# Second block, from mixing to feed-forward: work ordered by token tile

## The chip, the cores and the metric

The kernel runs on one core of one Trainium2 chip. The metric is the device time of one execution in microseconds, the median of several runs. TensorE (PE in the profile, PEld for its weight loads), VectorE (DVE), ScalarE (ACT) and GpSimd (POOL) compute; SyncE (SP) issues the transfers from the main memory.

## The reference

The program is two networks in a row on 256 tokens of width 1024. The first block (two layers with attention and a mixture of 32 experts) isn't touched. The second block ends like this, and only this part is touched:

```
merged = jnp.sum(gates * proj, axis=2)                 # (256, 1024)
x = x + rmsnorm(merged @ w_mix_out[l], post_mix_g[l])  # w_mix_out 1024 x 1024

h = rmsnorm(x, pre_ffn_g[l])
gt = causal_dwconv(h @ w_ff_gate[l], ff_conv_w[l]) + ff_conv_b[l]      # 1024 x 2816
y = (jax.nn.gelu(gt, approximate=True) * (h @ w_ff_up[l])) @ w_ff_down[l]
x = x + rmsnorm(y, post_ffn_g[l])
```

`rmsnorm(x, g)` is `x * rsqrt(mean(x * x) + 1e-6) * g`, over the 1024 features of each token. All of it is float32. The tokens are two tiles of 128, t = 0 and 1.

## The kernel before

**Split products.** A float32 matrix is split into a high part, rounded to the type float32r, and a low part, the rest (`split_into`, L266 for the cast on ACT and L269 for the subtraction on DVE or POOL). `mm` (L259 to L261) multiplies with three matmuls: high by high, high by low, low by high. Weights come as tiles of 1 MB (`W`, L302), which rotate through a ring of four. `W.tiles` splits such a tile into pieces of 128 x 1024, each into a pair of buffers of the pool `sp`; with six buffers three pairs rotate, and a pair is free again when its last matmul is through.

**Mixing.** `w_mix_out` is worked off in two halves of 512 columns. The merged activations `mT`, features on partitions, are the stationary operand and the weights move, 512 columns at a time: for each half 8 blocks k of 128 features, 2 token tiles, 3 matmuls, 96 in all, into four banks `pj`. In the second half `tail` asks for the blocks from the third on tile by tile: all of tile 0, then all of tile 1.

**The norms.** `post` takes the mean square of the four banks with Square on ACT (L1953), in the order half 0 tile 0, half 0 tile 1, half 1 tile 0, half 1 tile 1, then a root (L1955) and reciprocal (L1956) for each tile. For each tile DVE scales each half by that and by the gain row (L1963), and DVE or POOL adds it to X (L1964). Then each tile's X is squared (L1993); one root and one reciprocal serve both tiles (L1599, L1600). DVE writes X times that into `xn`, with the features re-ordered (L2000). `scaled_T` transposes it block by block on TensorE (L445), and ACT and DVE make from each transposed block, times the gain `g2`, the high and low part of `hT` (L1594, L1595).

**Feed-forward.** Six pieces of up to 512 columns of the gate and up weights in turn. In `fproj_g` the weights are the stationary operand, 128 columns at a time, and `hT` moves with all 256 tokens: 8 blocks k, 4 column groups, 3 matmuls, 96 a piece. Convolution and GELU follow on ACT and DVE, then the down projection, and `post` again, at the end of the program, with the output's transfers behind it.

**What sets the order.** The program is written as a plain sequence. A planner with its own model of the engines' times puts each engine's instructions into a queue: among the instructions that are ready in its reckoning it takes the one written first. TensorE, DVE and POOL follow the planner's queues; on ACT the instructions marked `pin` keep the written order among themselves. A tile of a pool that has the tag of another waits until that one's users are through.

Of the kernel before, what the change touches and what calls it, by code (L numbers as in the profile page):

```python
# [11 lines left out]
F32 = mybir.dt.float32  # L12
F32R = mybir.dt.float32r
# [5 lines left out]
D = 1024  # L19
# [144 lines left out]
def build(tc, A, out, stages=("A0", "M0", "A1", "M1", "F", "B"), dbg=None, inject=None):  # L164
# [22 lines left out]
    with es:  # L187
# [14 lines left out]
        def PS(tag="ps"):  # L202
            p, bufs = banks[-1]
            tag = one_bank[-1] if one_bank else tag
            tag = tag if tag in bufs else "ps"
            return p.tile([128, 512], F32, name=tag, tag=tag, bufs=bufs[tag])
# [5 lines left out]
        def pin(i, on=True):  # L212
            return tc.keep_in_program_order(i) if on and i is not None else i
# [235 lines left out]
        def t2(pool, dt=F32):  # L449
            return pool.tile([128, 512], dt, name="t2", tag="t2", bufs=t2n.get(id(pool), 6))  # L450
# [1094 lines left out]
        def block2():  # L1545
            with tc.tile_pool(name="blk", bufs=1, reuse_waits="tile") as B_, tc.tile_pool(name="splb", bufs=1, reuse_waits="tile") as sp:
                t2n[id(B_)] = 6
                esp = ExitStack()
                W.pools = [ringA] * 2 + [ringB] * (RN - 2)
                esp.enter_context(psum("ps_b1", ps=4, pj=4))  # L1550
# [393 lines left out]
                            if g == 2:  # L1944
                                split_into(mT[:, m:m + 2].rearrange("p a t -> p (a t)"), dst, pool_every=0)

                def post(row, pss, after, mid=lambda: None):
                    warm(AF.Sqrt)
                    ms = B_.tile([128, 2, 4], F32, name="pms", tag="pms", bufs=2)
                    for n in range(2):  # L1950
                        for t in range(2):
                            q0, q1, rs = (ms[:, t, i:i + 1] for i in range(3))
                            pin(S.activation(t2(B_), pss[t][n], AF.Square, accum_out=q1 if n else q0))  # L1953
                            if n:
                                pin(S.activation(rs, q1, AF.Sqrt, bias=q0, scale=1.0 / D))  # L1955
                                V.reciprocal(rs, rs)  # L1956
                            else:
                                V.tensor_scalar(q0, q0, 1.0 / D, 1e-6, op0=OP.mult, op1=OP.add)
                    for t in range(2):
                        for n in range(2):  # L1960
                            tmp = t2(B_)
                            cs = slice(512 * n, 512 * n + 512)
                            V.scalar_tensor_tensor(tmp, pss[t][n], ms[:, t, 2:3], row[:, cs], op0=OP.mult, op1=OP.mult)  # L1963
                            (V if n else G).tensor_add(X[:, t, cs], X[:, t, cs], tmp)  # L1964
                    mid()
                    for t in range(2):
                        after(t)

                def tail(lhs, parts, kn, last):
                    parts = list(parts)  # L1970
                    for late in range(2):
                        for t in range(2) if late else (None,):
                            for k, wk, cols in parts:
                                if (k >= kn - last) == late:
                                    for u in range(2) if t is None else (t,):
                                        for ps, cs in cols:
                                            mm(ps[u], lhs[:, k, 128 * u:128 * u + 128], wk[:, cs], k == 0, k == kn - 1)

                wm = A["w_mix_out_2"][0].rearrange("(k p) n -> p k n", p=128)
                row = L_.tile([128, D], F32, name="prow")  # L1980
                Q.dma_start(row, A["post_mix_g_2"].to_broadcast([128, D]))
                pss = []
                for n in range(2):
                    pss.append([PS("pj"), PS("pj")])
                    tail(mT, [(k, wk, [(pss[n], slice(0, 512))]) for k, wk in W(wm[:, :, 512 * n:512 * n + 512], 4).splits(sp)], 8, 6 * n)
                wfg = A["w_ff_gate_2"][0].rearrange("(p k) n -> p k n", k=8)
                wfu = A["w_ff_up_2"][0].rearrange("(p k) n -> p k n", k=8)
                xn = X[:, 2:4].rearrange("p t (k a) -> p t k a", k=8)
                ms = B_.tile([128, 2, 2], F32, name="nms")
                gate0 = W(wfg[:, :, 0:512], 4)  # L1990

                def after(t):
                    pin(S.activation(xn[:, t].rearrange("p a b -> p (a b)"), X[:, t], AF.Square, accum_out=ms[:, 0, t:t + 1]))  # L1993

                gate0.start(sp, 1)
                post(row, [[pss[n][t] for n in range(2)] for t in range(2)], after)
                inv_rms(ms[:, 1], ms[:, 0], 1.0 / D)
                gate0.more(1)
                for t in range(2):
                    V.tensor_scalar(xn[:, t], X[:, t].rearrange("q (p k) -> q k p", k=8), ms[:, 1, t:t + 1], None, op0=OP.mult)  # L2000
                debug("xmix", X)
                es2.close()
                L_ = es2.enter_context(tc.tile_pool(name="ffn", bufs=1, reuse_waits="tile"))
                hT = scaled_T(1, xn)
                yF = s2tile(L_, [128, 22, 256], "yF")
                for c in range(6):
                    n = min(512, 2816 - 512 * c)
                    pgs = fproj(W(wfg[:, :, 512 * c:512 * c + n], 4) if c else gate0, n)
                    pus = fproj(W(wfu[:, :, 512 * c:512 * c + n], 4), n)
                    for b in range(n // 256):  # L2010
                        pg, pu = pgs[b], pus[b]
                        y = t2(B_)
                        for a in range(2):
                            f = 4 * c + 2 * b + a
                            ya, ga = y[:, 256 * a:256 * a + 256], pg[:, 256 * a:256 * a + 256]
                            S.activation(ya, ga, AF.Identity, bias=vcol(66 + f), scale=vcol(44 + f))
                            V.scalar_tensor_tensor(ya[:, 1:], ga[:, :255], vcol(22 + f), ya[:, 1:], op0=OP.mult, op1=OP.add)
                            V.scalar_tensor_tensor(ya[:, 2:], ga[:, :254], vcol(f), ya[:, 2:], op0=OP.mult, op1=OP.add)
                        S.activation(y, y, AF.Gelu_apprx_tanh)
                        f = 4 * c + 2 * b  # L2020
                        V.tensor_mul(y, y, pu)
                        split_into(yF[:, f:f + 2].rearrange("p a t -> p (a t)"), y, pool_every=1)
                wd = A["w_ff_down_2"][0].rearrange("(k p) n -> p k n", p=128)
                row = L_.tile([128, D], F32, name="prow")
                Q.dma_start(row, A["post_ffn_g_2"].to_broadcast([128, D]))
                pss = [[PS("pj"), PS("pj")] for _ in range(2)]
                cols = [(pss[n], slice(512 * n, 512 * n + 512)) for n in range(2)]
# [106 lines left out]
```

## Time and profile before

| | |
|---|---|
| median of 3 runs | 2079.9 us (2075.26 to 2083.57) |
| profiled execution, own time | 2082.3 us |
| its span | 2080.6 us |
| mean granted TensorE clock | 0.975 |
| PE busy in the span | 1944.3 us (93%) |
| DVE / ACT / POOL busy | 1076.9 / 658.5 / 475.8 us |
| the second block, about | 1512 to the end |
| mixing matmuls end / first gate matmul | 1870.0 / 1883.5 us |

Times in the views are microseconds from the start of the span. A row of a timeline gives start, duration, engine, line, operation, what it writes and reads, shape, count, and in brackets how long the engine was idle before it and what ended that. The end of a matmul is modelled, and neighbouring matmuls overlap; their rate is read from start to start. Some matmul records are missing, so counts can be a little low.

### The profile page before, as it was taken

Reading aid. Unit: us, or ns where it says so; the run is one execution under the profiler, and the core shown is the slowest. Engines: PE = TensorE matmul, PEld = TensorE weight load, DVE = VectorE, ACT = ScalarE, POOL = GpSimd, SP = SyncE. Lnnn points to the kernel's source line nnn. Section 1 sums busy time; section 2 is a strip of 40 time slices with the busy share of each in tenths; the row PEclk is TensorE's granted clock in tenths of the full one; section 3 lists DMA queues with packets and bytes.
Section 4 is the critical chain, followed back from the end, with each engine's and each line's share of the span. In section 5 each row is a group of like instructions: output and inputs, shape, how many; then the busy total and the mean of one; then the engine's idle time right before and its main releaser. Section 6 shows DMA issues by size and latency. Waiting matters only on the chain. (4 is left out here: it accounts for less than half of the span.)

```text
span 2080.6 us, 29614 instructions
## 1 busy us (share of the span) xinstructions
PE 1944.3 (93%) x11353; PEld 1229.8 (59%) x11353; DVE 1076.9 (52%) x1919; ACT 658.5 (32%) x1188; POOL 475.8 (23%) x365
## 2 busy tenths in 40 slices
PE   6999999999899998999899997999989999998997
PEld 3755574444344444677743332333379998988996
DVE  3476674454426566746643231233366775446553
ACT  3355531101001114446511010111164444455553
POOL 1234321121213123210111010011131440332331
PEclk7999999999999999999899999999999999999999
DMA  8573338999999996642389999999864453554552
GB/s 316 209 258 128 102 134 339 398 427 426 427 426 425 427 423 251 246 142 102 132 364 427 426 427 427 426 426 427 370 223 135 146 182 129 183 192 142 183 189 95
DMA packets 137794, 585.44 MB, mean 281 GB/s; under 512 B 17257, under 2 KB 21863, under 8 KB 88367
## 3 DMA queue, kind: packets, MB, share of 16 engines
q1 hardware_dynamic: 136798, 583.47, 71.8%
q8 instruction: 92, 1.51, 0.3%
q14 instruction: 56, 0.45, 0.1%
q10 hardware_dynamic: 848, 0.01, 0.0%
HBM read 582.33 MB, written 1.11 MB: 280 GB/s over the span
## 5 line engine op out<-in xcount | busy, mean ns | idle before, releaser
L1216 PE MATMUL ps<-w,xt 128*64 128x512 f32 (+1 forms) x2232 | 430.1, 612 | 23.7 <-DMA w<-expert_w 23.4
L269 DVE TENSOR_TENSOR spl<-w,sph 128x1024 fp32r<-128x1024 f32 (+1 forms) x153 | 203.8, 1335 | 193.8 <-ACT sph L266 192.7
L266 ACT CAST sph<-w 128x1024 fp32r<-128x1024 f32 (+1 forms) x204 | 213.0, 1045 | 282.0 <-PE pj L260 258.2
L1216 PEld LDWEIGHTS ps<-w,xt 128*64 128x64 f32 (+1 forms) x2232 | 125.6, 127 | 276.0 <-issue 225.1
L1271 DVE SCALAR_TENSOR_TENSOR t<-ps,gt,t 128x512 fp32r<-128x512 f32 x52 | 39.1, 751 | 474.7 <-ACT t L1270 473.0
L1255 PE MATMUL ps<-w,t 128*64 128x512 f32 (+1 forms) x1128 | 257.1, 604 | 16.3 <-DMA w<-expert_w 13.5
L1287 POOL TENSOR_TENSOR X<-X,tm 128x512 f32<-128x512 f32 x78 | 106.1, 1360 | 687.8 <-DVE tm L1286 686.5
L259 PE MATMUL pj<-hT2h,sph 128*128 128x256 f32 x864 | 241.0, 283 | 0.0
L260 PE MATMUL pj<-hT2l,sph 128*128 128x256 f32 x864 | 240.4, 280 | 0.0
L261 PE MATMUL pj<-hT2h,spl 128*128 128x256 f32 x864 | 239.2, 281 | 0.3 <-DVE spl L269 0.3
L269 POOL TENSOR_TENSOR spl<-w,sph 128x1024 fp32r<-128x1024 f32 (+1 forms) x51 | 126.5, 2481 | 340.1 <-ACT sph L266 339.7
L1270 ACT ACTIVATE t<-ps,gt 128x512 fp32r<-128x512 f32 x52 | 35.7, 687 | 515.6 <-PE ps L1255 513.0
L1255 PEld LDWEIGHTS ps<-w,t 128*64 128x64 f32 (+1 forms) x1128 | 82.2, 125 | 183.1 <-issue 131.9
L260 PEld LDWEIGHTS pj<-hT2l,sph 128*128 128x128 f32 x864 | 163.0, 189 | 0.8 <-issue 0.7
L259 PEld LDWEIGHTS pj<-hT2h,sph 128*128 128x128 f32 x864 | 162.3, 189 | 1.2 <-issue 0.7
L261 PEld LDWEIGHTS pj<-hT2h,spl 128*128 128x128 f32 x864 | 161.7, 188 | 0.6 <-DVE spl L269 0.5
L1280 PE MATMUL ps<-t,sr 128*128 128x512 f32 x336 | 96.0, 415 | 9.2 <-DVE t L1271 7.5
L1286 DVE TENSOR_TENSOR tm<-ps,s 128x512 f32<-128x512 f32 x156 | 101.9, 680 | 1.4 <-PE ps L1280 1.3
L1280 PEld LDWEIGHTS ps<-t,sr 128*128 128x128 f32 x336 | 60.1, 188 | 57.4 <-ACT t L1270 22.3
L445 PEld LDWEIGHTS ps<-c,t 128*128 128x128 f32 x496 | 56.1, 141 | 52.5 <-issue 20.0
L1287 DVE TENSOR_TENSOR X<-X,tm 128x512 f32<-128x512 f32 x78 | 85.6, 1097 | 1.9
L445 PE MATMUL ps<-c,t 128*128 128x128 f32 x496 | 76.2, 280 | 7.8 <-DVE t L1228 2.9
(509 smaller groups left out, 3394.1 us busy)
## 6 DMA issues: line engine op xcount, KB each, us to landing
w<-expert_w SPq DMA_DIRECT2D x372, 1024.0 KB
w<-ada_w SPq DMA_DIRECT2D x48, 1024.0 KB
w<-w_in SPq DMA_DIRECT2D x30, 1024.0 KB
w<-diff_w_in SPq DMA_DIRECT2D x12, 1024.0 KB
X<-expert_w SPq DMA_DIRECT2D x12, 1024.0 KB
w<-w_gate SPq DMA_DIRECT2D x12, 1024.0 KB
w<-w_ff_down SPq DMA_DIRECT2D x11, 1024.0 KB
w<-w_ff_gate SPq DMA_DIRECT2D x10, 1024.0 KB
```

The source lines that it names most:

```text
L259: T.matmul(o, l.hi, r.hi, start=start, stop=False, **kw)
L260: T.matmul(o, l.hi, r.lo, start=False, stop=False, **kw)
L261: T.matmul(o, l.lo, r.hi, start=False, stop=stop, **kw)
L266: pin(S.copy(d.hi, src), pinned)
L269: eng.tensor_tensor(d.lo, src, d.hi.bitcast(F32), op=OP.subtract)
L445: T.transpose(o, i, ident[:i.shape[0], :i.shape[0]])
L1216: T.matmul(ps[m * q:m * q + m, :], xt[:, k, off + m * q:off + m * q + m], at(w, k)[k], start=(k == 0), stop=(k == 7))
L1255: T.matmul(ps[m * q:m * q + m, :], hT_[:, k, m * q:m * q + m], at(w, k)[k, slice(512 * jo, 512 * jo + 512)], start=(k == 0), stop=(k == 3))
L1271: V.scalar_tensor_tensor(yl, ps, gt[:, 0:1], yh.bitcast(F32), op0=OP.mult, op1=OP.subtract)
L1280: T.matmul(ps, sr[:, 128 * t:128 * t + 128], ys[jo][q], start=(q == 0), stop=(q == 1))
L1286: V.tensor_mul(tmp, ps, grow[:, t // 2, cs])
L1287: (G if jo else V).tensor_add(X[:, t, cs], X[:, t, cs], tmp)
```

## The change

- The pool of the second block's splits has eight buffers (four pairs) instead of six.
- The second half's mixing weights are split into places of their own: three new pairs of tiles and the pair of tiles `ys`, free by then. Only the first four blocks of the first half are multiplied for both tiles in turn; the rest, 4 blocks of the first half and 8 of the second, is written for tile 0 and then for tile 1.
- `post` is written tile by tile, and `after(t)` follows each tile's additions. This holds for its second call, at the end, too.
- After mixing, `after(t)` squares the tile's X, takes its own root and reciprocal, and scales the identity by it into `dg`. A float32 matmul with a block of X (every eighth column) as stationary and `dg` as moving operand takes the place of normalising and transposing. DVE multiplies four blocks at a time with the gain, and `split_into` makes the two parts of `hT` (cast on ACT, subtraction on DVE).
- The first gate piece is multiplied by `fproj_by_tile`: all blocks for tile 0, then for tile 1, with 128 moving columns each. Its first two pieces of weights are split ahead of `post` (before: one).
- The gain rows use the place of an earlier tile, tag `sc`, both the same one.

```diff
                 t2n[id(B_)] = 6
+                pool_bufs[id(sp)] = 8
...
-                def post(row, pss, after, mid=lambda: None):
+                def post(row, pss, after):
                     warm(AF.Sqrt)
                     ms = B_.tile([128, 2, 4], F32, name="pms", tag="pms", bufs=2)
-                    for n in range(2):
-                        for t in range(2):
-                            q0, q1, rs = (ms[:, t, i:i + 1] for i in range(3))
-                            pin(S.activation(t2(B_), pss[t][n], AF.Square, accum_out=q1 if n else q0))
-                            if n:
-                                pin(S.activation(rs, q1, AF.Sqrt, bias=q0, scale=1.0 / D))
-                                V.reciprocal(rs, rs)
-                            else:
-                                V.tensor_scalar(q0, q0, 1.0 / D, 1e-6, op0=OP.mult, op1=OP.add)
                     for t in range(2):
+                        q0, q1, rs = (ms[:, t, i:i + 1] for i in range(3))
+                        pin(S.activation(t2(B_), pss[t][0], AF.Square, accum_out=q0))
+                        V.tensor_scalar(q0, q0, 1.0 / D, 1e-6, op0=OP.mult, op1=OP.add)
+                        pin(S.activation(t2(B_), pss[t][1], AF.Square, accum_out=q1))
+                        pin(S.activation(rs, q1, AF.Sqrt, bias=q0, scale=1.0 / D))
+                        V.reciprocal(rs, rs)
                         for n in range(2):
                             tmp = t2(B_)
                             cs = slice(512 * n, 512 * n + 512)
...
                             (V if n else G).tensor_add(X[:, t, cs], X[:, t, cs], tmp)
-                    mid()
-                    for t in range(2):
                         after(t)
...
-                row = L_.tile([128, D], F32, name="prow")
+                row = B_.tile([128, 2 * D], F32, name="prow", tag="sc")[:, :D]
                 Q.dma_start(row, A["post_mix_g_2"].to_broadcast([128, D]))
-                pss = []
-                for n in range(2):
-                    pss.append([PS("pj"), PS("pj")])
-                    tail(mT, [(k, wk, [(pss[n], slice(0, 512))]) for k, wk in W(wm[:, :, 512 * n:512 * n + 512], 4).splits(sp)], 8, 6 * n)
+                pss = [[PS("pj"), PS("pj")] for _ in range(2)]
+                w0, w1 = (W(wm[:, :, 512 * n:512 * n + 512], 4) for n in range(2))
+                late = []
+                for k, wk in w0.splits(sp):
+                    if k < 4:
+                        for t in range(2):
+                            mm(pss[t][0], mT[:, k, 128 * t:128 * t + 128], wk, k == 0, False)
+                    else:
+                        late.append((0, k, wk))
+                for i in range(4):
+                    if i:
+                        d = S2(*(L_.tile([128, 4, 256], F32R, name=f"wm{i}{x}") for x in "hl"))
+                    else:
+                        d = s2tile(L_, [128, 4, 256], "ys")
+                    d = d.rearrange("p a b -> p (a b)").rearrange("p (k n) -> p k n", k=2)
+                    split_into(d, w1.t[i // 2][:, 2 * (i % 2):2 * (i % 2) + 2], 2)
+                    late += [(1, 2 * i + j, d[:, j]) for j in range(2)]
+                for t in range(2):
+                    for n, k, wk in late:
+                        mm(pss[t][n], mT[:, k, 128 * t:128 * t + 128], wk, k == 0, k == 7)
...
                 gate0 = W(wfg[:, :, 0:512], 4)
+                gate0.start(sp, 2)
                 def after(t):
-                    pin(S.activation(xn[:, t].rearrange("p a b -> p (a b)"), X[:, t], AF.Square, accum_out=ms[:, 0, t:t + 1]))
-                gate0.start(sp, 1)
-                post(row, [[pss[n][t] for n in range(2)] for t in range(2)], after)
-                inv_rms(ms[:, 1], ms[:, 0], 1.0 / D)
-                gate0.more(1)
-                for t in range(2):
-                    V.tensor_scalar(xn[:, t], X[:, t].rearrange("q (p k) -> q k p", k=8), ms[:, 1, t:t + 1], None, op0=OP.mult)
+                    pin(S.activation(X[:, 2 + t], X[:, t], AF.Square, accum_out=ms[:, 0, t:t + 1]))
+                    inv_rms(ms[:, 1, t:t + 1], ms[:, 0, t:t + 1], 1.0 / D)
+                    V.tensor_scalar(dg[:, t], ident, ms[:, 1, t:t + 1], None, op0=OP.mult)
+                    xv = X[:, t].rearrange("q (p k) -> q k p", k=8)
+                    for k in range(0, 8, 4):
+                        ps = PS()
+                        for a in range(4):
+                            T.matmul(ps[:, 128 * a:128 * a + 128], xv[:, k + a], dg[:, t], start=True, stop=True)
+                        f = t2(B_).rearrange("p (k t) -> p k t", k=4)
+                        V.tensor_tensor(f, ps.rearrange("p (k t) -> p k t", k=4),
+                                        g2[:, 1, k:k + 4, None].to_broadcast([128, 4, 128]), op=OP.mult)
+                        split_into(hT[:, k:k + 4, 128 * t:128 * t + 128], f, 0)
+                post(row, pss, after)
...
-                hT = scaled_T(1, xn)
+                def fproj_by_tile(w):
+                    ps2 = [PS("pj"), PS("pj")]
+                    held = []
+                    for t in range(2):
+                        for k, wk in held if t else w.splits(sp):
+                            if not t:
+                                held.append((k, wk))
+                            for c in range(4):
+                                o = 256 * (c % 2) + 128 * t
+                                mm(ps2[c // 2][:, o:o + 128], wk[:, 128 * c:128 * c + 128], hT[:, k, 128 * t:128 * t + 128],
+                                   k == 0 and c % 2 == 0 and t == 0, k == 7, skip_group_check=True)
+                    return ps2
...
-                    pgs = fproj(W(wfg[:, :, 512 * c:512 * c + n], 4) if c else gate0, n)
+                    pgs = fproj(W(wfg[:, :, 512 * c:512 * c + n], 4), n) if c else fproj_by_tile(gate0)
```

## Rows read from the trace of the kernel before

**Rows 1.** Windows: stretch, length, busy us (instructions) by engine, clock, DMA.

```profile
1852.00:1870.50 18.50, 18.42 (x82) 14.92 (x80) 8.34 (x10) 9.78 (x17) 3.17 (x2) 1.00 0.68 234
1870.50:1883.50 13.00, 2.06 (x8) 1.43 (x8) 10.80 (x12) 5.89 (x11) 5.20 (x3) 0.70 0.10 24
1950.00:2000.00 50.00, 50.00 (x427) 50.00 (x426) 28.36 (x37) 27.17 (x35) 15.78 (x8) 1.00 0.50 164
```

**Rows 2.** Timeline of PE from the last mixing matmuls to the gate piece.

```profile
1870.03 0.39 PE L261 MATMUL pj<-sph,mTl 128*128 128x512 f32 x1
1878.94 0.66 PE L445 MATMUL ps<-c,X 128*128 128x128 f32 x2 [8.53 <-DVE X L2000]
1882.10 1.51 PE L445 MATMUL ps<-c,X 128*128 128x128 f32 x6 [2.49 <-DVE X L2000]
1883.53 0.80 PE L259 MATMUL pj<-hT2h,sph 128*128 128x256 f32 x2
...
1886.37 0.60 PE L445 MATMUL ps<-c,X 128*128 128x128 f32 x4
```

**Rows 3.** Timeline of ACT and DVE in the same stretch.

```profile
1869.32 0.60 ACT L1953 ACTIVATE t<-pj 128x512 f32<-128x512 f32 x1 [0.77 <-PE pj L261]
...
1870.57 1.41 DVE L1963 SCALAR_TENSOR_TENSOR t<-pj,pms,prow 128x512 f32<-128x512 f32 x2
...
1872.02 1.20 DVE L1964 TENSOR_TENSOR X<-X,t 128x512 f32<-128x512 f32 x1
...
1873.31 1.06 ACT L1993 ACTIVATE X<-X 128x1024 f32<-128x1024 f32 x1 [1.84 <-DVE X L1964]
...
1877.04 0.29 ACT L1599 ACTIVATE nms<-nms,epsc 128x2 f32<-128x2 f32 x1
...
1877.64 4.31 DVE L2000 TENSOR_SCALAR X<-X,nms 128x1024 f32<-128x1024 f32 x2
```

**Rows 4.** Windows of about a microsecond: the granted clock around the seam.

```profile
1874.00:1875.00 1.00, 0.00 (x0) 0.00 (x0) 0.96 (x2) 0.46 (x2) 1.00 (x1) 1.00 0.00 0
...
1884.50:1885.50 1.00, 1.00 (x6) 1.00 (x6) 0.85 (x3) 0.48 (x2) 0.00 (x0) 0.50 0.85 330
...
1886.50:1890.00 3.50, 3.50 (x33) 3.50 (x32) 1.34 (x2) 2.26 (x4) 0.00 (x0) 1.00 0.02 5
```

**Rows 5.** PE timeline of L402 and L440; L440 by line: ns least, median, most.

```profile
110.06 1.84 PE L402 MATMUL ad<-c,R 128*128 128x2 f32 x16
...
800.56 1.48 PE L440 MATMUL ps<-c,R 128*64 128x4 f32 x11
...
L440 PE MATMUL ps<-c,R x64: 261/261/283, 34.4 to 803.9; 128*64 128x4 f32 x64
```

**Rows 6.** Windows: the granted clock under the first run of L440.

```profile
34.40:35.40 1.00, 0.97 (x8) 0.97 (x9) 0.00 (x0) 0.00 (x0) 0.00 (x0) 1.00 1.02 416
...
36.40:37.30 0.90, 0.90 (x11) 0.90 (x10) 0.00 (x0) 0.00 (x0) 0.00 (x0) 0.50 1.04 405
```

**Rows 7.** Timeline of ACT and of the transfer queue during mixing.

```profile
1859.35 1.05 ACT L266 CAST sph<-w 128x1024 fp32r<-128x1024 f32 x1 [1.67 <-PE pj L260]
...
1826.45 17.44 SPq L302 DMA_DIRECT2D w<-w_mix_out  x4
```

**Rows 8.** Timeline of DVE and ACT ahead of mixing: half-tile work of 512 columns.

```profile
1847.95 1.48 DVE L1942 TENSOR_TENSOR t<-t,pj 128x512 f32<-128x512 f32 x2 [2.71 <-PE pj L261]
...
1851.52 1.78 DVE L269 TENSOR_TENSOR mTl<-mF,mTh 128x512 fp32r<-128x512 f32 x1
...
1854.36 0.68 DVE L269 TENSOR_TENSOR mTl<-mF,mTh 128x512 fp32r<-128x512 f32 x1
...
1852.79 0.62 ACT L266 CAST mTh<-mF 128x512 fp32r<-128x512 f32 x1 [0.55 <-POOL mF L1943]
```

**Rows 9.** Timeline of ACT and DVE at the end of the program.

```profile
2069.61 0.60 ACT L1953 ACTIVATE t<-pj 128x512 f32<-128x512 f32 x1 [0.22 <-PE pj L261]
...
2070.20 0.59 ACT L1953 ACTIVATE t<-pj 128x512 f32<-128x512 f32 x1
...
2071.44 1.41 DVE L1963 SCALAR_TENSOR_TENSOR t<-pj,pms,prow 128x512 f32<-128x512 f32 x2
```

More of the change, by code (lines that the diff above doesn't have):

```diff
@@ L1962, in post @@
                             cs = slice(512 * n, 512 * n + 512)
-                            V.scalar_tensor_tensor(tmp, pss[t][n], ms[:, t, 2:3], row[:, cs], op0=OP.mult, op1=OP.mult)
+                            V.scalar_tensor_tensor(tmp, pss[t][n], rs, row[:, cs], op0=OP.mult, op1=OP.mult)
                             (V if n else G).tensor_add(X[:, t, cs], X[:, t, cs], tmp)
-                    mid()
-                    for t in range(2):
                         after(t)
@@ L1986, in block2 @@
+                for t in range(2):
+                    for n, k, wk in late:
+                        mm(pss[t][n], mT[:, k, 128 * t:128 * t + 128], wk, k == 0, k == 7)
                 wfg = A["w_ff_gate_2"][0].rearrange("(p k) n -> p k n", k=8)
                 wfu = A["w_ff_up_2"][0].rearrange("(p k) n -> p k n", k=8)
-                xn = X[:, 2:4].rearrange("p t (k a) -> p t k a", k=8)
                 ms = B_.tile([128, 2, 2], F32, name="nms")
+                dg = B_.tile([128, 2, 128], F32, name="dg")
@@ L1990, in block2 @@
+                hT = s2tile(B_, [128, 8, 256], "hT2")
                 gate0 = W(wfg[:, :, 0:512], 4)
+                gate0.start(sp, 2)
                 def after(t):
-                    pin(S.activation(xn[:, t].rearrange("p a b -> p (a b)"), X[:, t], AF.Square, accum_out=ms[:, 0, t:t + 1]))
-                gate0.start(sp, 1)
-                post(row, [[pss[n][t] for n in range(2)] for t in range(2)], after)
-                inv_rms(ms[:, 1], ms[:, 0], 1.0 / D)
-                gate0.more(1)
@@ L2023, in block2 @@
                 wd = A["w_ff_down_2"][0].rearrange("(k p) n -> p k n", p=128)
-                row = L_.tile([128, D], F32, name="prow")
+                row = B_.tile([128, 2 * D], F32, name="prow", tag="sc")[:, :D]
                 Q.dma_start(row, A["post_ffn_g_2"].to_broadcast([128, D]))
```

## The prediction

> **What bounds the kernel now.** I read the windows by stage first. From 1852 to 1870.5 us and from 1950 to 2000 TensorE is busy all the time at full clock [rows 1]; in between, from 1870.5 to 1883.5, it works 2.06 of 13 us. So everything around the change is bounded by TensorE, except one seam: the chain from the last mixing matmul to the first gate matmul. The timeline of PE gives the seam its size [rows 2]: the last mixing matmul starts at 1870.03, PE waits 8.53 us, does two transposes, waits 2.49 us more, and starts the gate piece at 1883.53. Counted from start to start, and leaving each matmul its normal slot, PE loses 8.7 + 2.7 + 0.3 = 11.7 us there.
>
> The timeline of ACT and DVE says what fills the seam [rows 3]: two squares, a root, then for each of two token tiles 1.4 us of scaling, 1.2 us of adding and 1.06 us of squaring, one common root at 1877.04, and 4.31 us in which DVE writes both normalised tiles before the second transposes can go. The same rows show that the first tile is hardly ahead: its last Square starts at 1869.32, released by PE, only 0.7 us before PE's last start, though the loop asks for the first tile's matmuls ahead of the second's. The planner filled waits for split weights with the second tile.
>
> The clock, by windows [rows 4]: still full in 1874 to 1875, after 4 us of idle; 0.50 (1.2 GHz) in 1884.5 to 1885.5; full again in 1886.5 to 1890. From 1883.53 to about 1885.7 a 256-column matmul takes 0.21 us instead of the 0.117 (427 in 50 us [rows 1]): ten matmuls, 1.0 us lost. Eight of the sixteen transposes ran at half clock too, 0.11 us lost on each, 0.8. What the seam costs in all: 11.7 + 1.8 = 13.5 us. That is the most that the change can win back there.
>
> **The change, part by part.**
>
> *Mixing.* The 96 matmuls stay, at 0.225 us (82 records in 18.42 us [rows 1]). Eight splits stay also, but those of the second half go to places of their own. Today a split waits for PE to give a buffer back, about every 2.7 us; the row shows 1.67 us of waiting for PE before a cast, and four in a row are like it [rows 7]. Without that wait they can be early: the four transfers of the mixing weights are issued between 1826.45 and 1844 [rows 7], and ACT needs 1.05 us for each cast. Then the first tile's last 36 matmuls end 36 x 0.225 = 8.1 us before the second's. The cost on PE is nothing; the cover is that all splits are ready by about 1861, and without it the planner mixes the tiles again (rival A).
>
> *Chain of the first tile.* After its last matmul: Square to second add, 1869.32 to 1873.22 in the rows [rows 3], 3.9 us; Square of X 1.06 and its read-out; root and reciprocal 0.6 (1877.04 to 1877.64); the small diagonal tile `dg`, not in the trace, between 0 and the 0.74 of 512 columns [rows 8], by its 128 columns 0.2; with hand-overs 6.1 us. Against 8.1 us of head start it ends before PE is through with mixing.
>
> *Products instead of transposes.* Sixteen transposes at 0.11 leave (four in 0.60 [rows 2]), 1.75 us. Sixteen float32 products come, whose stationary operand is X read at every eighth element. The nearest row with such a stationary operand is L440: 64 columns, one every (1.48 - 0.26) / 10 = 0.12 us; 128 columns make 0.24. The lower bound is a plain 128-column load with two columns to compute, L402, at 0.11 [rows 5]. I take 0.24: 3.84 us, so +2.1 us (bounds 0 and +2.1, and above it as much again if the moving columns came on top: +3.9).
>
> *Behind them.* For each half tile: the multiplication by g2 on DVE (0.74 as in L1942), a cast 0.62, a subtraction 0.68 to 1.8, the lower where nothing else is in its way [rows 8], 2.0 us to the first usable operand. In return the 4.31 us of L2000 go, and the two passes over every transposed pair. For the first tile this falls just behind the end of mixing: PE waits 0 to 1.4 us there. The second tile's chain needs 6.1 us plus some 3 us in which DVE is at work for the first, so until about 1879.5, then 2 us more; it lies beside the first tile's 10.7 us of gate matmuls. A wait remains only if the planner puts the second tile's products into PE's queue too soon: 0 to 3.5 us. I take 1.4 us for both waits. Then 12.1 of 13.5 us come back; the clock stays up, since it outlived 4 us of idle [rows 4].
>
> *First gate piece by tile.* Here the gain is paid out. 96 matmuls of 256 columns become 192 of 128 columns, each with a load of its own. The trace has no such matmul in the split type. From below: half of the present slot, 0.06. From above: as 128 columns at half clock, 0.22 (transposes, six in 1.51 us at 0.50 [rows 2, 4]). The nearest row is the load itself, L402: 0.11 per 128 columns although only two columns are computed [rows 5], so loads bound it. 192 x 0.111 = 21.3 us against 96 x 0.1175 = 11.3: +10.0 us.
>
> The Trainium skill ("TensorE: Matmul & The Clock Gate", section "Back-to-back issue gap") gives about 81 ns a matmul for a sustained stream with 128 columns. By it, as an estimate, the piece would take 15.6 us, 5.7 fewer than I take; no run here shows that rate.
>
> *Wider split pool.* Eight buffers instead of six in the whole second block. Where six are in use PE has no idle time (50.00 of 50 us [rows 1]), so nothing. All four pairs of the gate piece are held until its second pass; the next piece's first split then has 72 x 0.111 = 8 us, for a cast of 1.05 [rows 7] and a subtraction about as long.
>
> *Row moved.* The second gain row takes the place of the first, so its DMA, and what SP has behind it, waits until about 1876. The weights behind it are those of the third piece, needed 96 x 0.1175 us after the up piece starts, at about 1908, and the queue takes some 4.4 us for a megabyte (17.44 for four [rows 7]). Nothing.
>
> *End of the program.* The same chain stands at the end. There ACT squares the second tile (2069.61) before the first tile's second half (2070.20), and scaling starts at 2071.44 [rows 9]. With the new order the first tile's root comes 0.7 us earlier; if the fourth buffer pair lets the first tile really be ahead, both its scalings and its add (2.6 us) go below the last matmuls. From 0 to -2.5 us, taken as -1.2.
>
> **Sum.** -12.1 (seam and clock) + 2.1 (products) + 10.0 (gate piece) - 1.2 (end) = -1.2 us. The profiled execution took 2082.3 us (span 2080.6 and 1.7 around it), 2.4 above the median of the runs, 2079.9. From the median: 2078.7 us. I say **2079**: no change that can be measured; below half a per cent (10.4 us) a difference of this kernel is not told from none.
>
> **Rivals.**
>
> *A. The head start doesn't come.* If splits come late in the planner's reckoning, PE takes the second tile early, as it does now [rows 3]. Then the first chain's 6.1 us and 2 us behind it stand open: PE waits about 8 us instead of 1.4, and 6.6 us are missing: 2079 + 6.6, about **2085**. For it: the loop already asks for this order and the rows don't show it. Against it: now three pairs of buffers rotate, then the eight splits have eight places.
>
> *B. The piece by tile runs at half speed (the other side).* Place: the 192 matmuls. Their array work is half of what it was while the loads set the pace, and the clock can fall under such a stream: at L440, four columns a matmul, PE is busy throughout and the granted clock goes from 1.00 to 0.50 within 3 us [rows 6]. If a matmul then costs 0.22, 192 x 0.11 = 21 us come on top: **2100**. It decides from 0.171 us a matmul on (11.6 / 192 above 0.111). Against it: 128 columns are not four, and L440 itself keeps its pace.
>
> *C. Loads are cheaper than the rows say.* Next to a matmul of the split type a load may be hidden better than in L402. Halfway to the lower bound, at 0.085 a matmul, 5 us fewer; with products at their lower bound and the full gain at the end 3.4 more: **2074 to 2070**, and at 0.06 2069 or less. For it: the present slot of 0.1175 is about what 256 columns alone need at 2.4 GHz (0.107), so no row shows the load of this type as the bound. Against it: L402 sits at 0.11 with next to nothing to compute. The 81 ns of the Trainium skill's page "TensorE: Matmul & The Clock Gate" ("Back-to-back issue gap") would lie here.
>
> **How the numbers follow.** Forecast 0.54 (its own range 2074 to 2084), A 0.20, B 0.10, C 0.11, and 0.05 for a planner that orders the rest of the block otherwise, to either side. Below 2069 lies 0.08, mostly from C, above 2092 0.10, all of B. Range 2069 to 2092. Faster than 2069.5: 0.08; slower than 2090.3: 0.13, B and what of A is worse than worked out; the rest within.
>
> **What would show it.** Right: the wait of 8.53 us before the first product gone; granted clock 1.00 through the seam; products 0.24 apart; gate matmuls with 128 columns 0.11 apart and some 21 us long; the first up matmul no more than 2 us from where it is today (about 1897); the last ACT Squares in tile order. Wrong: gate matmuls at 0.08 or at 0.2, a clock of 0.50 between 1872 and 1895, the first tile's last Square again released just before the end of mixing, or a PE wait of over 3 us before the second tile's products.

## The result, and the profile after

The changed kernel takes 2093.99 us (median of 11 runs, 2091.98 to 2109.6) against 2080.0 for the kernel before in the same session (11 runs): ratio 1.0077, 95% interval 1.0062 to 1.0093. It is **slower by 0.8%**: the interval excludes 1. The run of 2109.6 us had a mean granted clock of 0.967, the other ten, 2092.0 to 2095.7 us, 0.973 to 0.980; it left no trace. The profiled execution took 2095.67 us, span 2094.0 (before: 2080.6). Forecast were 2079 and at most 2092, so the prediction was wrong.

To see where the 13.4 us of span come from, I cut each trace at the same four instructions: the last expert matmul, the first and the last mixing matmul, and the last matmul of the program. Stages in us:

| kernel | to mixing | mixing | seam and feed-forward | end | sum |
|---|---|---|---|---|---|
| before | 337.5 | 21.6 | 199.6 | 11.0 | 569.7 |
| after | 340.5 | 22.9 | 210.9 | 8.4 | 582.6 |

The differences are +3.0, +1.3, +11.3 and -2.6, together 12.9 us; the other 0.4 us lie ahead of the last expert matmul. The timeline of PE in the changed kernel shows each of them (columns: start, length, engine, line, operation, out<-in, shapes, count; in brackets idle time ahead and what ended it):

```profile
1728.34 0.52 PE L445 MATMUL ps<-c,pd 128*128 128x128 f32 x3 [1.52 <-DVE pd L1882]
1730.71 0.52 PE L445 MATMUL ps<-c,pd 128*128 128x128 f32 x3 [1.18 <-DVE pd L1882]
...
1859.48 0.50 PE L260 MATMUL pj<-ysl,mTh 128*128 128x512 f32 x1 [0.65 <-DVE ysl L269]
...
1874.70 0.39 PE L261 MATMUL pj<-wm3h,mTl 128*128 128x512 f32 x1
...
1875.61 4.06 PE L2014 MATMUL ps<-dg,X 128*128 128x128 f32 x16 [0.53 <-DVE dg L2009]
...
1881.06 0.33 PE L260 MATMUL pj<-hT2l,sph 128*128 128x128 f32 x1 [1.21 <-DVE hT2l L269]
...
1883.66 0.41 PE L259 MATMUL pj<-hT2h,sph 128*128 128x128 f32 x1
...
1896.03 4.02 PE L2014 MATMUL ps<-dg,X 128*128 128x128 f32 x16
...
1899.81 0.31 PE L260 MATMUL pj<-hT2l,sph 128*128 128x128 f32 x1
...
1912.79 0.33 PE L259 MATMUL pj<-hT2h,sph 128*128 128x256 f32 x1
```

The 8.53 us ahead of the first transposes [rows 2] are gone: 0.53 stands in their place. But the eight products of a tile appear as 16 instructions, two for each product, which take 4.0 us together. The gate piece lies between 1881 and 1912.8, and its matmuls last longer before 1899 than after. The windows tell why (columns as in [rows 1]):

```profile
1874.90:1880.00 5.10, 4.42 (x19) 4.12 (x18) 1.43 (x4) 0.67 (x2) 0.00 (x0) 1.00 0.63 206
1880.00:1882.00 2.00, 0.94 (x8) 0.94 (x9) 1.76 (x4) 1.56 (x4) 0.00 (x0) 1.00 0.00 0
1882.00:1884.00 2.00, 2.00 (x12) 2.00 (x12) 1.32 (x3) 0.51 (x3) 0.33 (x1) 0.51 0.03 8
1887.00:1890.00 3.00, 3.00 (x16) 3.00 (x16) 0.45 (x2) 0.07 (x1) 0.00 (x0) 0.50 0.01 3
1896.00:1899.00 3.00, 3.00 (x15) 3.00 (x14) 0.69 (x1) 0.01 (x1) 0.00 (x0) 0.50 0.00 0
1902.00:1905.00 3.00, 3.00 (x30) 3.00 (x28) 0.16 (x1) 0.16 (x1) 0.00 (x0) 1.00 0.00 0
```

The granted clock is 0.50 (1.2 GHz) from 1882.0 to 1899.1, although PE is busy all that time. 66 of the 192 gate matmuls start in it, 0.213 us apart; the others stand 0.112 apart. The last view is that of ACT and DVE, at the seam and at the end:

```profile
1868.32 0.60 ACT L1955 ACTIVATE t<-pj 128x512 f32<-128x512 f32 x1 [1.58 <-PE pj L261]
...
1875.18 0.29 DVE L2009 TENSOR_SCALAR dg<-c,nms 128x128 f32<-128x128 f32 x1
...
1880.44 0.62 ACT L266 CAST hT2h<-t 128x512 fp32r<-128x512 f32 x1 [1.30 <-DVE t L2016]
1880.96 0.59 ACT L1953 ACTIVATE t<-pj 128x512 f32<-128x512 f32 x1
...
2083.95 1.41 DVE L1961 SCALAR_TENSOR_TENSOR t<-pj,pms,prow 128x512 f32<-128x512 f32 x2
2085.30 0.60 ACT L1953 ACTIVATE t<-pj 128x512 f32<-128x512 f32 x1 [1.58 <-PE pj L261]
```

Tile 0's last Square starts 6.4 us before the last mixing matmul (before: 0.7 us [rows 3]): the head start is there. From that Square to the end of the row of `dg`, tile 0's chain takes 7.2 us, where 6.1 were reckoned. Tile 1's Square could start at about 1875, but ACT's queue has tile 0's cast ahead of it, which waits for the products; it starts at 1880.96. At the end tile 0 is scaled before tile 1 is squared, where before both tiles were squared first [rows 9].

### The profile page after: what moved, and what is told of

Its sections match the earlier page's. It is cut to its first block, busy times and chain, and to the rows that moved or that the text cites. A ratio compares the mean times of both kernels' runs of the same rounds, so it can differ in the third digit from the quotient of the medians.

```text
span 2094.0 us, 29811 instructions
## 1 busy us (share of the span) xinstructions
PE 1964.0 (94%) x11465; PEld 1249.2 (60%) x11465; DVE 1078.8 (52%) x1919; ACT 655.9 (31%) x1184; POOL 480.6 (23%) x366
## 4 chain that ended last, share of the span: by engine, by line
PE 64%; DMA 26%; DVE 5%; ACT 3%; issue 1%; SPq 0%; POOL 0%; ACTq 0%; DVEq 0%; POOLq 0%
DMA w<-expert_w 22%; PE pj L259 11%; PE pj L260 11%; PE pj L261 11%; PE ps L1216 9%; PE ps L1255 4%; PE ps L445 3%; PE ps L1280 2%; DMA X<-expert_w 2%; PE ad L357 2%; PE ps L1098 2%; PE ps L1099 1%; DMA w<-ada_w 1%; PE ps L765 1%; PE pj L803 1%
## 5 line engine op out<-in xcount | busy, mean ns | idle before, releaser
L266 ACT CAST sph<-w 128x1024 fp32r<-128x1024 f32 (+1 forms) x200 | 208.7, 1046 | 274.7 <-PE pj L260 241.4
L259 PE MATMUL pj<-hT2h,sph 128*128 128x256 f32 (+1 forms) x896 | 256.3, 287 | 0.0
L260 PE MATMUL pj<-hT2l,sph 128*128 128x256 f32 (+1 forms) x896 | 253.2, 283 | 1.2 <-DVE hT2l L269 1.2
L261 PE MATMUL pj<-hT2h,spl 128*128 128x256 f32 (+1 forms) x896 | 252.9, 283 | 0.0
L260 PEld LDWEIGHTS pj<-hT2l,sph 128*128 128x128 f32 x896 | 171.3, 191 | 2.8 <-issue 1.4
L259 PEld LDWEIGHTS pj<-hT2h,sph 128*128 128x128 f32 x896 | 171.5, 192 | 1.5 <-issue 1.2
L261 PEld LDWEIGHTS pj<-hT2h,spl 128*128 128x128 f32 x896 | 171.5, 192 | 0.0
```

What stands on the lines that cost most here:

```text
L259: T.matmul(o, l.hi, r.hi, start=start, stop=False, **kw)
L260: T.matmul(o, l.hi, r.lo, start=False, stop=False, **kw)
L261: T.matmul(o, l.lo, r.hi, start=False, stop=stop, **kw)
L266: pin(S.copy(d.hi, src), pinned)
```

## The experiments

My theory after the result: the pool costs 3 us ahead of mixing, the 128-column piece 10, the products 6 instead of 2, and their strided loads let the clock fall, 7 more. Rivals are given with each run. Long edits are shown shortened. The stages of all runs, cut as above, and their medians beside the kernel before of the same session:

| run | to mixing | mixing | seam, feed-forward | end | sum | median us | ratio (interval) |
|---|---|---|---|---|---|---|---|
| e1_pool8 | 341.1 | 21.6 | 201.0 | 10.9 | 574.5 | 2086.9 | 1.0031 (1.0021-1.0041) |
| e2_gate256 | 340.5 | 22.9 | 201.3 | 8.4 | 573.1 | 2084.9 | 1.0020 (1.0008-1.0031) |
| e3_contig | 340.0 | 22.7 | 200.1 | 8.4 | 571.3 | 2084.5 | 1.0019 (1.0009-1.0029) |
| e4_fill | 340.5 | 22.9 | 208.6 | 8.4 | 580.4 | 2092.8 | 1.0050 (1.0033-1.0068) |
| e5_narrow | 337.1 | 24.3 | 210.3 | 8.4 | 580.1 | 2093.1 | 1.0063 (1.0050-1.0077) |
| e6_post | 337.6 | 21.6 | 202.7 | 10.3 | 572.2 | 2081.5 | 1.0009 (0.9996-1.0021) |
| e7_full | 337.7 | 24.1 | 198.3 | 8.4 | 568.4 | 2080.3 | 1.0005 (0.9994-1.0015) |
| e8_bytile | 337.7 | 25.8 | 205.1 | 8.4 | 577.0 | 2090.5 | 1.0054 (1.0039-1.0068) |
| e9_seam | 337.6 | 22.1 | 194.3 | 8.4 | 562.4 | 2074.0 | 0.9973 (0.9962-0.9985) |
| e10_piece | 337.7 | 21.6 | 230.4 | 10.9 | 600.5 | 2112.3 | 1.0150 (1.0137-1.0163) |

**The pool alone** (e1_pool8), on the kernel before:

```diff
+                pool_bufs[id(sp)] = 8
```

> The kernel before, with eight split buffers instead of six in the whole second block, and nothing else of the change. The changed kernel starts mixing 3.4 us later than the kernel before (1851.84 against 1848.47), 2.9 us of it idle time of TensorE in the second block's attention that the kernel before doesn't have. Theory (the wider pool lets the planner put splits ahead of the attention's small steps): mixing starts 3 us later here too, and the time is 2083 us less what the fourth pair gives at the end of the program; if the end's gain of 2.6 us comes from the pair, about 2080.5. Rival (the shift comes from the rewritten end of the block, or from chance): mixing starts within 0.5 us of the kernel before, 2080.

The timeline of PE in this run, in the second block's attention:

```profile
1727.23 0.52 PE L445 MATMUL ps<-c,pd 128*128 128x128 f32 x3 [1.51 <-DVE pd L1882]
```

In the kernel before, the transposes of `pd`, a tile of the attention, have no wait ahead of them at that place:

```profile
1727.05 0.60 PE L445 MATMUL ps<-c,pd 128*128 128x128 f32 x4
...
1731.14 0.49 PE L445 MATMUL ps<-c,pd 128*128 128x128 f32 x3
```

So the wait is that of the changed kernel, and mixing starts 3.6 us later than before. The end stage stays at 10.9: four pairs alone do not bring the gain there. The median, 2086.9, is 4 us above the theory's 2083. The seam takes 1.4 us more as well: its stretch at a granted clock of 0.50 lasts 13.7 us in this trace and 10.2 in that of the kernel before. Why it is longer was not tested.

**The gate piece at full width** (e2_gate256), on the changed kernel:

```diff
-  pgs = ... if c else fproj_by_tile(gate0)
+  pgs = fproj(W(wfg[...], 4) if c else gate0, n)
```

> The changed kernel with the first gate piece in full width again (256 columns, 96 matmuls); the rest of the change stays. Theory (the piece by tile costs more than the wait that it fills: 126 matmuls at 0.112 and 66 at 0.213 instead of 96 at 0.1175): PE waits some 9 to 10 us for the second tile, then 11.3 us of gate matmuls and 1 us for the clock, so that the up piece starts 11 to 14 us earlier than in the changed kernel: 2080 to 2083 us. Rival (what is lost lies in the wider pool, the products and the mixing, and by tile pays for itself): 2094 or more.

PE in this run:

```profile
1868.92 4.06 PE L2014 MATMUL ps<-dg,X 128*128 128x128 f32 x16 [0.53 <-DVE dg L2009]
...
1881.03 4.10 PE L2014 MATMUL ps<-dg,X 128*128 128x128 f32 x16 [8.05 <-DVE dg L2009]
```

Now PE waits 8.05 us for tile 1's `dg`, and the low clock is back at 1.00 10.2 us after it fell. In spite of that wait the stages are 9.5 us shorter than in the changed kernel: the piece by tile costs more than the wait that it fills. The median, 2084.9, is 2 us above the expected range.

**Contiguous stationary operand** (e3_contig), the weights' rows being dealt out so that block k is 128 neighbouring columns of X:

```diff
-  "(p k) n -> p k n"                      (wfg, wfu; the gain likewise)
+  "(k p) n -> p k n"
-  xv = X[:, t].rearrange("q (p k) -> q k p", k=8)
+  xv = X[:, t].rearrange("q (k p) -> q k p", k=8)
```

> The changed kernel with the features of the feed-forward weights and of the gain in contiguous blocks, so that the products' stationary operand is read in one piece. Theory (the strided loads make the products slow, two passes of 0.24 each, and their sparse work on the array together with the gap behind them lets the clock fall): passes 0.11 apart, 32 of them 3.6 instead of 7.7 us; granted clock 1.00 through the first tile's gate matmuls, all of them 0.112 apart: 2094 - 4.1 - 6.7 = 2083 us. Rival (the stream of 128-column matmuls pulls the clock down by itself): products as fast, but 0.50 in the gate piece again, 2090 us.

PE, then the windows:

```profile
1877.06 2.02 PE L2014 MATMUL ps<-dg,X 128*128 128x128 f32 x16 [0.53 <-DVE dg L2009]
```

```profile
1885.00:1890.00 5.00, 5.00 (x47) 5.00 (x47) 0.53 (x3) 1.45 (x3) 0.00 (x0) 1.00 0.26 88
1895.00:1900.00 5.00, 5.00 (x47) 5.00 (x46) 1.23 (x1) 2.09 (x2) 0.57 (x1) 1.00 0.01 3
```

The products halve, 2.02 us a tile, and the clock stays at 1.00 through the whole piece. Of the stage 10.7 us come back: 4 from the products, 6.7 from the clock. The ten runs lie between 2082.9 and 2086.4, near the theory's 2083 and not the rival's 2090.

**Fillers** (e4_fill): the products stay strided; between them go matmuls with 512 columns, which nobody reads:

```diff
+  if a % 2 == 0:
+      T.matmul(pss[t][0], dg[:, t], X[:, t, 0:512], start=True, stop=True)
```

> The changed kernel with extra work for the array: a 512-column float32 matmul (two passes) whose result nobody reads, ahead of every second product, four per tile. Theory (the clock falls because the products and the gap behind them leave the array mostly idle): granted clock 1.00 through the gate piece, all 192 matmuls 0.112 apart, 6.7 us won; the fillers cost at most 8 x 0.43 = 3.4 us, less what the products' loads hide: 2087 to 2092 us. Rival (the 128-column stream pulls the clock down): 0.50 again in the first tile's gate matmuls, 2094 to 2098 us.

```profile
1875.00:1880.00 5.00, 4.57 (x16) 3.53 (x17) 0.98 (x2) 0.20 (x1) 0.00 (x0) 1.00 0.63 210
1885.00:1890.00 5.00, 5.00 (x47) 5.00 (x46) 2.95 (x5) 1.71 (x4) 1.28 (x1) 1.00 0.30 103
```

```profile
1877.19 1.02 PE L2015 MATMUL pj<-X,dg 128*128 128x512 f32 x2
```

In these windows the clock stays at 1.00 and all gate matmuls stand 0.112 apart. There is more work on PE, and yet the stage is 2.3 us shorter; the median, 2092.8, is just above the expected range. The fillers cost more than was reckoned: each is two instructions 0.43 us apart, so eight take 6.9 us instead of 3.4. So the gate piece alone doesn't make the clock fall: two separate edits to the products, which leave the piece as it is, take the fall away. Both also shorten the wait between the products and the piece: 1.21 us in the changed kernel, 0.54 and 0.41 in e3, none in e4. Slow products and the wait behind them are not told apart by these two runs.

**The pool back to three pairs** (e5_narrow), on the changed kernel; from mixing on, a fourth pair comes from a tag of its own:

```diff
-  pool_bufs[id(sp)] = 8
+  tag, nb = ("sq", 2) if W.wide and i % 4 == 3 else ("sp", pool_bufs.get(id(pool), 6))
```

> The changed kernel with six split buffers up to the mixing and two more, under a tag of their own, from there on (every fourth pair uses them). Nothing else is undone. Theory (part of the loss comes from the wider pool ahead of the mixing): mixing starts 337.5 us after the last matmul of the experts, as in the kernel before, instead of 340.5, the idle time of 1.52 and 1.18 us in the attention is gone, and the time is 3 us below the changed kernel, 2091. Rival (the shift has another cause): as the changed kernel, 2094.

The 3.4 us ahead of mixing come back, but mixing loses 1.4: PE there waits 2.35 us for `ysl` instead of 0.65. The stages are 2.5 us shorter in all; the median, 2093.1 where 2091 was expected, did not move beyond the noise. The products are strided here too, with a wait of 1.21 us behind them, and the granted clock is 0.50 from 1880.4 to 1897.4, as long as in the changed kernel.

**`post` by tile alone** (e6_post), on the kernel before:

```diff
-  for n in range(2):
-      for t in range(2):
-          ... Square, and after both tiles' squares the two roots
+  for t in range(2):
+      ... Square, Square, Sqrt, reciprocal; both scalings and adds; after(t)
```

> The kernel before with the changed order inside post alone: each tile's squares, root, scaling and adds together, for both calls. Theory (the gain at the end of the program, 11.0 us from the last matmul's start to the end of the span before and 8.4 in the changed kernel, comes from this order): 8.5 us here too, little else, 2078 us. Rival (it needs the fourth buffer pair, so that the first tile really finishes ahead): 10.3 us and 2080.

The end gains 0.7 only and comes to the rival's 10.3; the median is 2081.5 where the theory had 2078. The seam loses 3.1: ACT's queue has tile 0's Square of X ahead of tile 1's squares, which start at 1875.58, and the transposes still wait for both tiles. PE:

```profile
1883.20 0.66 PE L445 MATMUL ps<-c,X 128*128 128x128 f32 x2 [11.56 <-DVE X L1995]
```

Neither the order (10.3) nor the pair (10.9) brings the 8.4 at the end; all runs with both have it.

**All repairs, full width** (e7_full): e3's layout, e5's pool, e2's gate, and the chain cut into parts that are issued in turn:

```diff
+  stats(0); apply(0); stats(1); finish(0); apply(1); finish(1)
```

> The changed kernel with the pool of e5_narrow, the contiguous products of e3_contig, the gate piece in full width as in e2_gate256, and the second tile's squares written ahead of the first tile's products, whose casts follow them in ACT's order. Theory: from the last mixing matmul to the last matmul of the program e2_gate256 took 201.3 us and the kernel before 199.6; both tiles' products are 2 us shorter, the second tile's squares come 5 us earlier, since in e2_gate256 ACT holds them behind a cast that waits for the products: 194 to 196. With 8.4 us at the end instead of 11.0, and 1.3 more for mixing: 2074 to 2077 us. Rival (the clock, low after the wait, eats it): 2080.

The median is 2080.3 instead of 2074 to 2077; that is the rival's number. What remained is seen in PE and DVE:

```profile
1855.16 0.50 PE L260 MATMUL pj<-ysl,mTh 128*128 128x512 f32 x1 [2.24 <-DVE ysl L269]
...
1879.46 3.75 PE L2028 MATMUL ps<-dg,X 128*128 128x128 f32 x16 [6.71 <-DVE dg L2021]
```

```profile
1851.71 3.40 DVE L269 TENSOR_TENSOR ysl<-w,ysh 128x1024 fp32r<-128x1024 f32 x1
1855.03 3.48 DVE L269 TENSOR_TENSOR mTl<-mF,mTh 128x512 fp32r<-128x512 f32 x2
...
1873.39 1.40 DVE L1965 SCALAR_TENSOR_TENSOR t<-pj,pms,prow 128x512 f32<-128x512 f32 x2
1874.71 1.92 DVE L269 TENSOR_TENSOR hT2l<-t,hT2h 128x512 fp32r<-128x512 f32 x2
1876.55 0.68 DVE L1966 TENSOR_TENSOR X<-X,t 128x512 f32<-128x512 f32 x1
```

Both waits are made by DVE's order: mixing's first split stands late, and tile 1's add behind tile 0's two subtractions. The rival's cause has a part too: the granted clock is 0.50 from 1875.1 to 1885.3, and tile 1's contiguous products take 3.75 us where tile 0's take 2.02. With the first gate matmuls that is about 2.6 us (15 passes at 0.10 and 11 matmuls at 0.096 over their time at full clock).

**The same with the piece by tile** (e8_bytile), on e7:

```diff
-  pgs = fproj(W(wfg[...], 4) if c else gate0, n)
+  pgs = fproj(W(wfg[...], 4), n) if c else fproj_by_tile(gate0)
```

> As e7_full, but with the gate piece by tile. Theory (a matmul of 128 columns costs 0.112 us, nearly the 0.1175 of 256 columns, so the second tile's pass alone lasts as long as the whole piece in full width, and the first tile's pass pays only as far as it fills a wait): e7_full waits some 6 us for the second tile, this one not at all but works 10.7 us longer; 3 to 5 us slower than e7_full, 2078 to 2081. Rival (the wait in e7_full with its low clock is worth the whole pass): same as e7_full or faster.

```profile
1881.89 0.33 PE L260 MATMUL pj<-hT2l,sph 128*128 128x128 f32 x1 [2.35 <-DVE hT2l L269]
```

```profile
1880.00:1883.50 3.50, 1.61 (x14) 1.61 (x15) 3.04 (x4) 0.36 (x1) 1.26 (x1) 1.00 0.39 150
1883.80:1888.00 4.20, 4.20 (x21) 4.20 (x21) 0.45 (x2) 0.78 (x3) 0.00 (x0) 0.50 0.00 0
1890.60:1895.00 4.40, 4.40 (x42) 4.40 (x41) 2.56 (x4) 1.24 (x2) 0.00 (x0) 1.00 0.00 0
```

The median is 10.2 us above that of e7, where 3 to 5 were expected. Here the products are contiguous, yet after a wait of 2.35 us of PE the clock falls all the same, at 1883.7; 22 gate matmuls and then nine passes of tile 1's products run 0.213 apart, about 3.1 us lost. So strided products are not needed for the fall.

The seam stage is 6.8 us longer than in e7: 10.2 for the width, 3.8 less of waiting (7.0 in e7, 3.2 here, where none was expected), and about 0.5 more for the clock, 3.1 against 2.6. Another 1.7 us lie in mixing, where this trace has a granted clock of 0.50 for 3.4 us behind the wait for `ysl`.

**DVE's order written out** (e9_seam): e7, the last pair of mixing weights in `ys` instead of the first, and tile 1's chain ahead of tile 0's subtractions:

```diff
-  if i:
+  if i < 3:
...
+  products(0)
+  with in_order(["V"]):
+      stats(1); scale(1); norm(1); gained(0); gained(0); diag(1)
```

> As e7_full (gate piece in full width, contiguous products, six buffers up to the mixing), with two more edits: of the second half's split mixing weights the last pair, not the first, takes the place of ys; and at the seam DVE does the second tile's scaling, adding and diagonal tile ahead of the first tile's subtractions, in written order. Theory (what was left in e7_full are two waits that DVE's order makes: 2.24 us in mixing, where the subtraction for ys stands ahead of those for mT, and about 4 of the 6.71 us before the second tile's products): mixing 21.8 us long instead of 24.1, the wait before the second tile's products 3 to 4 us, granted clock 1.00 all through, from the last mixing matmul to the last of all 193 to 195; 2074 to 2076 us. Rival (the order moves, but the planner or the clock takes it back): 2079 to 2081.

PE, then the windows:

```profile
1869.75 1.95 PE L2035 MATMUL ps<-dg,X 128*128 128x128 f32 x16
...
1876.07 3.39 PE L2035 MATMUL ps<-dg,X 128*128 128x128 f32 x16 [4.37 <-DVE dg L174]
```

```profile
1870.00:1876.30 6.30, 1.93 (x18) 1.77 (x17) 4.77 (x9) 3.27 (x8) 1.26 (x1) 1.00 0.64 232
1876.60:1879.80 3.20, 3.20 (x16) 3.06 (x15) 1.97 (x5) 0.62 (x1) 0.00 (x0) 0.50 0.00 0
1880.00:1883.00 3.00, 3.00 (x26) 3.00 (x27) 1.15 (x2) 0.93 (x2) 0.00 (x0) 1.00 0.02 5
```

2074.0 us (7 runs), ratio 0.9973 to the kernel before, interval 0.9962 to 0.9985: less than the half per cent that I had named as telling from no change, but more runs stand behind it and the interval excludes 1. It beats both kernels. Nothing waits for `ysl` and tile 1's wait is 4.37. The clock was expected to stay at 1.00; it is at 0.50 for 3.4 us, from 1876.5 to 1879.9.

**The piece alone** (e10_piece), on the kernel before, transposes and all:

```diff
   hT = scaled_T(1, xn)
-  pgs = fproj(W(wfg[...], 4) if c else gate0, n)
+  pgs = fproj(W(wfg[...], 4), n) if c else fproj_by_tile(gate0)
+  tag, nb = ("sq", 2) if W.wide and i % 4 == 3 else ("sp", pool_bufs.get(id(pool), 6))
```

> The kernel before with the first gate piece by tile and nothing else (an extra pair of split buffers from there on, since the piece holds all four pairs). Both tiles are ready here before the piece starts, so it can win nothing: its price stands alone, and it starts at half clock, as in the kernel before. Theory: 192 x 0.112 = 21.5 us for 11.3, +10.2 at full clock; and at half clock a matmul takes 0.213, whatever made the clock fall, until it rises: if 128 columns bring it back as soon as 256 did (2.3 us), +11: 2091 us. Rival (a stream of 128 columns at half clock doesn't bring the clock back for long, as in the changed kernel, where it took 17 us): the first tile's pass and more at 0.213, +18 to +21: 2097 to 2101 us.

```profile
1884.50:1926.90 42.40, 42.40 (x200) 42.38 (x200) 6.40 (x11) 6.94 (x11) 2.36 (x1) 0.50 0.22 75
1927.00:1930.00 3.00, 3.00 (x15) 3.00 (x15) 2.42 (x5) 1.97 (x3) 0.00 (x0) 0.50 0.00 0
1931.00:1940.00 9.00, 9.00 (x79) 9.00 (x78) 5.17 (x7) 5.61 (x7) 0.00 (x0) 1.00 0.52 171
```

The seam of before drops the clock, as in [rows 4]. There ten 256-column matmuls later it was full again; here it stays at 0.50 through all 192 matmuls of 128 columns, PE being busy 42.40 of 42.40 us, and rises only when the next piece's 256-column matmuls run. It is the rival's mechanism, and dearer than it said: 31 us in the stage instead of 18 to 21. All 192 matmuls run slow, not the first pass and some more: 192 x (0.213 - 0.112) = 19.4 us on top of the 10.2 for the width, and the start of the next piece runs slow too.

## Why the prediction was wrong

The terms of its sum against the traces (us):

| term | predicted | measured |
|---|---|---|
| dead time at the seam | -10.3 (11.7, 1.4 left) | -9.6 (2.1 left) |
| clock at the seam | -1.8 | +4.9 (6.7 lost, 1.8 before) |
| products for transposes | +2.1 | +5.9 |
| gate piece at full clock | +10.0 | +10.2 |
| ahead of mixing | 0 | +3.0 |
| mixing | 0 | +1.3 |
| end | -1.2 | -2.6 |

Measured they add to 13.1 us; the stages have 12.9 of the span's 13.4. The clock's 6.7 are 66 x (0.213 - 0.112); the gate's 10.2 are 192 x 0.112 - 11.3; the products' 5.9 are 32 x 0.24 - 1.75.

**"The clock stays up, since it outlived 4 us of idle"** is the step that failed most. I read idle time alone. What stood ahead of the fall at 1882.0 was 4 us of strided products and then short waits (1.21 us and less). With contiguous products (e3) or fillers among strided ones (e4) the clock stayed up; that is shown. Whether the products or the wait behind them did it is not: both edits shortened the wait too, and in e8 a longer one (2.35 us) brought the fall behind contiguous products. Rival B had the price, 21 us for a whole piece at 0.22, but the wrong trigger: a 128-column stream alone doesn't pull the clock down. It ran at 1.00 for 20 us (e3), and at 0.50 it stayed at 0.50 for 42 (e10). Where the clock fell soon after the stream's start (1.0 us in the changed kernel, 1.8 in e8), products and waits stood ahead of it. Because the low clock held for 66 matmuls only, the loss was a third of B's.

The run of 2109.6 us would fit a low clock that lasts through the remaining 126 gate matmuls as well: 126 x 0.101 = 12.7 us, an estimate from the spacings above. Without a trace of that run it is not shown.

What lifts the clock at 1899.1 stays open: in the changed kernel, e5 and e8 the rise came during tile 1's products, which are plain float32, or at their end, but no run isolates that. Nor is it settled why the 2.3 us wait in mixing drops the clock in e8 and not in e5 and e7, or what in e8's seam dropped it and in e3's did not: the last wait before the stream is 2.35 us in e8 and 0.41 in e3, but no run changes that alone.

**The products** were mis-sized. Each strided pass costs 0.24, as worked out from L440; but a float32 matmul of 128 columns is two instructions. The rows could have told it [rows 5]: L440 has 64 records for the 32 matmuls that the code writes. The upper bound, +3.9, was meant for another reason and was also too low.

**"Wider split pool: nothing"** failed. It was argued from a stage in which PE has no idle time; the cost came in another, the attention, some 120 us ahead of mixing, where PE came to wait 1.5 and 1.2 us for `pd`, which DVE makes (e1: the same waits with this one line; e5: gone without it).

**Mixing** was costed at nothing on condition that all splits are ready. The first of the new places, `ys`, wasn't (`ysl` is its low part); 0.65 of the 1.3 us is the wait on `ysl`. Moving it to the last pair (e9) brought mixing to 22.1.

**Right** were the gate piece at full clock (rate by L402, +10.2 against +10.0), the end (its bound of -2.5 was reached, by order and buffers together, as e6 and e1 apart show), and the head start, by which rival A falls: with 6.4 us for 8.1 and a chain of 7.2 for 6.1 it was smaller than reckoned, yet the wait ahead of the products stayed at 0.53. Rival C falls too: no stream of 128-column matmuls ran faster than 0.112 us each. The 81 ns of the Trainium skill ("TensorE: Matmul & The Clock Gate", "Back-to-back issue gap") were not seen; 0.112 was, in every stretch of the piece by tile at full clock.

Even with all of it mended, the idea of the piece by tile doesn't pay: a 128-column matmul costs nearly as much (0.112) as a 256-column one (0.1175), so tile 1's pass alone takes nearly as long as the whole piece did (10.8 us against 11.3), and tile 0's pass is worth something only as far as PE would wait. e8 against e7 shows it: 10.2 us of extra matmuls in the seam for 3.8 us less of waiting, with about the same loss to the clock in both.

## What to carry to other kernels

Before a matmul stream is cut into narrower matmuls, look for the spacing of the narrow ones in the trace: where 128 columns take 0.112 us and 256 take 0.1175, half the columns cost nearly the whole time, and a wait of 7 us isn't worth 10 us of extra matmuls. Look also at what runs just before and just after a place where the clock may fall, since a stream that keeps PE busy without bringing the clock back, as the 128-column one did in e10, turns one dip into a long one. And a buffer count is a change to the whole planned stretch: read its cost from the stages ahead of the one that it was meant for.

## What was not expected of the hardware

- A PE that is busy in every record can stay at half clock: 42.4 us at 0.50 with 128-column matmuls (e10). The Trainium skill ("TensorE: Matmul & The Clock Gate", "What's actually happening") says that the clock follows how busy the PE has been recently; here a PE without an idle moment in the trace stayed at the lower level.
- At half clock a 128-column matmul of the split type takes 0.213 us instead of 0.112.
- A pass over a stationary operand with every eighth column takes 0.24 us at either clock: 4.06 us for 16 at full clock in the changed kernel, and 0.24 apart as well for tile 1's 16 in e5, all at 0.50; contiguous it takes 0.11 at full clock (1.95 and 2.02 for 16) and 0.21 at half (3.75 for 16, e7). The strided pass kept its time at both levels, the contiguous one did not.
- A plain float32 product is two instructions, a split-type one is one; with 512 columns each of the two takes 0.43 us (e4), a split-type one 0.225.
